# The product with w_out by seven block products in place of eight

## The chip, the cores and the metric

The kernel runs on one core of a Trainium2 chip. The metric is the device time of one launch in microseconds (us). Three runs of the kernel before took 3358.61, 3364.39 and 3369.11 us, a median of 3364.39 us. The engines are TensorE (PE: matmuls, with weight loads shown as PEld), VectorE (DVE), ScalarE (ACT), GpSimd (POOL) and SyncE (SP, which issues the DMAs).

## The reference

One layer of a diffusion backbone: a gated DeltaNet mixer on 2048 tokens of 1024 channels, then a channel mixer, then a final norm. The change lies in the channel mixer, whose hidden width is 2816 = 22 tiles of 128 channels:

```python
def conv_glu(h, w_in, conv_w, conv_b, w_out):
    val, gate = jnp.split(h @ w_in, 2, axis=-1)
    gate = dw_conv(gate, conv_w) + conv_b            # three taps along the tokens
    return (val * jax.nn.silu(gate)) @ w_out

x_lat = x_lat + mod_l[5] * conv_glu(h_lat, ffn_w_in[i], ffn_conv_w[i], ffn_conv_b[i], ffn_w_out[i])
return rms_norm(x_lat, final_norm_g)
```

All of it is float32. The kernel multiplies float32 matrices by splitting each operand into a rounded part and a remainder and adding three matmuls (`mm3`, L837): hi·hi, hi·lo and lo·hi.

## The kernel before

**Order of the work.** Every operation is recorded with its engine, an assumed cost, a priority and the buffer slots it takes (`Plan.op`). A list scheduler then writes out one order for each engine, from assumed costs and latencies; each engine runs its list in that order and waits at each instruction for its data and buffers. A late instruction so holds all that stands behind it on its engine.

**Forming an operand** (`form`, L1739) is a cast on ScalarE (L1752, the rounded part) and a subtraction on VectorE or GpSimd (L1755, the remainder). Formed stationary tiles take one of seven `wf` slots, moving operands one of fourteen `bf` slots; raw loads take one of four `raw3` slots, strictly in the order of recording (`load3`).

**The two windows of hidden channels** (`ffn_window`). A window is 1024 tokens. It goes over 11 pairs g of channel tiles. Each pair takes seven gate products (convolution and silu follow) and then seven value products; a product is 12 matmuls into one PSUM bank. The seven products already replace eight block products: `channels` (L1830) forms seven sums of weight blocks, four of them by GpSimd combines (L1850), and `products3` (L1861) adds the results. In the order of its VectorE instructions: the addition of the second product (`big<-fps,pc`, L1957), two additions that make u2 and u4 (`pc<-fps,pc`, L1904), one that makes u3, and then L1957 three times. The first of these three frees the bank of the third product, which the seventh product uses again. After a pair's value products GpSimd multiplies value by silu(gate) in two instructions of 1024 tokens (L2002), and SP stores both to DRAM (`hid_d`, L2005).

**The product with w_out** (`ffn_out`). For each half of the 1024 output columns and for blocks of four tiles of 128 tokens (the last block of the second half in two pieces), it runs over the 11 pairs: two formed channel tiles of the block (`wf`), times the two formed weight tiles (`bf`), added in four PSUM banks. A step of one channel tile on four token tiles is 12 matmuls. The weights of a half are formed once, in its first block. The first half is scaled, added to the residual and stored (`half_out`); the second adds its own half, takes the norm of the row and writes the output (`finish_out`).

Of the kernel before, what the change touches and what calls it, by code (L numbers as in the profile page):

```python
# [18 lines left out]
P = 128  # L19
# [227 lines left out]
class Kernel:  # L247
# [7 lines left out]
    def setup(self):  # L255
# [6 lines left out]
        self.hid_d = [dp.tile([P, 2, SEQ], F32, name=f"hid_d{g}") for g in range(NF // 2)]  # L262
        self.comb_d = [[dp.tile([P, 4, WB], F32, name=f"comb_d{w}{k}") for k in range(4)] for w in range(2)]
        self.y_d = [dp.tile([P, WB], F32, name=f"y_d{c}") for c in range(SEQ // P)]
# [1413 lines left out]
    def plan3(self):  # L1678
# [5 lines left out]

        nc, pl = self.nc, self.plan
# [36 lines left out]
        self.hid_done = {}  # L1722
# [208 lines left out]
    def ffn_window(self, w):  # L1931
# [12 lines left out]
        def hidden(g, prio):  # L1944
# [46 lines left out]
            vals = [[], []]  # L1991
            V = self.channels(g, 0, prio - 20)
            self.products3(V, B, prio, block_put(v_, v0), vals)
            for f in range(2):
                def ends(f=f):
                    if w:
                        nc.gpsimd.tensor_copy(v_[f].t[:, 0:1], carry(f, 2, 3))
                    else:
                        nc.gpsimd.tensor_copy(carry(f, 2, 3), v_[f].t[:, N - 1:N])

                def times(f=f):
                    nc.gpsimd.tensor_tensor(v_[f].t[:, :n], v_[f].t[:, :n], a_[f].t[:, :n], ALU.mult)  # L2002

# [4 lines left out]
                a = pl.op("POOL", 2.4, times, [e, acts[f]], prio, uses=[v_[f], a_[f]])  # L2008
                self.hid_done.setdefault(w, []).append(pl.op("SP", 1.5, store, [a], prio, uses=[v_[f]]))
# [3 lines left out]

    def ffn_out(self):


        nc, pl, T = self.nc, self.plan, self.ffn_t
        TT, TS = nc.vector.tensor_tensor, nc.vector.tensor_scalar
        base = 3000
        m5, fg, junk = (Buf("braw") for _ in range(3))  # L2020
        flat = lambda b: b.t.rearrange("p a b -> p (a b)")
# [9 lines left out]
        a = pl.op("SP", 1.0, load_m5, self.m_done[1] + [self.b_load, self.open_c], base - 40, alloc=[m5, fg])  # L2031
# [3 lines left out]
        n_acc = 0  # L2035
        y_done = {}
        nj = NF // 2
        for half in range(2):
            ns = slice(half * WB, (half + 1) * WB)
            W = []  # L2040
            blocks = [[0, 1, 2, 3], [4, 5, 6, 7], [8, 9, 10, 11]] + ([[12, 13], [14, 15]] if half else [[12, 13, 14, 15]])
            for i, ts in enumerate(blocks):
                prio = base + 1000 * half + 100 * i
                t0, nt = ts[0] * P, len(ts)
                ps = [Buf((("inv", "inv", "sc", "sc"), ("zp", "zp", "tr", "tr"))[n_acc % 2][t]) for t in range(nt)]
                n_acc += 1
                a = None
                for j in range(nj):
                    p = prio + j - 25
                    if i == 0:  # L2050
                        raw, l = self.load3(
                            "raw3", [P, 2, WB], self.i["ffn_out"][2 * j:2 * j + 2, :, ns].rearrange("f p c -> p f c"), [], p
                        )
                        W.append(self.form(lambda raw=raw: raw.t, [2, WB], raw, [l], p, "bf", "DVE" if j % 2 else "POOL"))
                    deps = self.hid_done[0] + (self.hid_done[1] if t0 + nt * P > 2 * WB - 1 else [])
                    raw, l = self.load3("raw3", [P, 2, nt * P], self.hid_d[j][:, :, t0:t0 + nt * P], deps, p)
                    hids = [
                        self.form(lambda raw=raw, f=f: raw.t[:, f], [nt * P], raw, [l], p, "wf", "DVE") for f in range(2)
                    ]

                    def mms(f, j=j, hids=hids, ps=ps, nt=nt, W=W):
                        if j == 0 and f == 0:
                            for b in ps:
                                b.t = self.pp.tile([P, WB], F32, name="fy", tag=b.tag, bufs=2)
                        h, w = hids[f].t, W[j].t
                        for t in range(nt):
                            s = slice(t * P, (t + 1) * P)
                            self.mm3(
                                ps[t].t, h[:, 0, s], h[:, 1, s], w[:, 0, f, :], w[:, 1, f, :],
                                j == 0 and f == 0, j == nj - 1 and f == 1,  # L2070
                            )

                    for f in range(2):
                        first = j == 0 and f == 0
                        a = pl.op(
                            "PE", 0.684 * nt, lambda f=f, mms=mms: mms(f), [a, W[j].done, hids[f].done], prio + j,
                            alloc=ps if first else [], uses=[W[j], hids[f]] + ([] if first else ps),
                        )
                    if j == nj - 5:
                        near = a  # L2080
                for t, c in enumerate(ts):
                    if half == 0:
                        y_done[c] = self.half_out(prio + 20, c, ps[t], a, near, m5, m5_done)
                    else:
                        self.finish_out(prio + 20, c, ps[t], a, near, m5, fg, junk, [m5_done, fg_done, new_junk], y_done[c], i > 2)

    def half_out(self, prio, c, ps, done, near, m5, m5_done):
# [4 lines left out]
        def load():  # L2092
            self.new3(row, [P, D])
            nc.sync.dma_start(row.t[:, WB:], self.x1_d[c][:, :WB])

        l = pl.op("SP", 0.8, load, [near, self.x1_done[c]], prio - 10, alloc=[row])
        a = pl.op("DVE", 0.67, lambda: nc.vector.tensor_tensor(
            row.t[:, :WB], ps.t, m5.t[:, :WB], ALU.mult), [l, done, m5_done], prio, uses=[row, ps, m5])
        a = pl.op("POOL", 1.25, lambda: nc.gpsimd.tensor_tensor(
            row.t[:, :WB], row.t[:, :WB], row.t[:, WB:], ALU.add), [a], prio, uses=[row])  # L2100
        return pl.op("SP", 0.8, lambda: nc.sync.dma_start(self.y_d[c], row.t[:, :WB]), [a], prio, uses=[row])

    def finish_out(self, prio, c, ps, done, near, m5, fg, junk, ready, y_done, late):

        nc, pl = self.nc, self.plan
        row, tmp, st = Buf("big3"), Buf("pc"), Buf("st3")
        TS = nc.vector.tensor_scalar

        def load():
            self.new3(row, [P, D])  # L2110
            nc.sync.dma_start(row.t[:, :WB], self.y_d[c])
            nc.sync.dma_start(row.t[:, WB:], self.x1_d[c][:, WB:])

        def scaled():
            self.new3(tmp, [P, WB])
            nc.vector.tensor_tensor(tmp.t, ps.t, m5.t[:, WB:], ALU.mult)

        def square(k):
            if k == 0:
                self.new3(st, [P, 4])  # L2120
            s = slice(k * WB, (k + 1) * WB)
            nc.scalar.activation(junk.t[:, s], row.t[:, s], AF.Square, accum_out=st.t[:, k:k + 1])

        eng, add = ("DVE", nc.vector) if late else ("POOL", nc.gpsimd)
# [81 lines left out]
```

## Time and profile before

| | us |
|---|---|
| median of three runs | 3364.39 |
| the profiled execution | 3358.7 |
| its span, first to last instruction | 3357.0 |
| first matmul of the windows' products (`fps`) | 1985.6 |
| window 2 begins its products | 2439.0 |
| first matmul of the product with w_out | 2859.9 |
| last matmul of it starts | 3346.2 |

The profiled execution is 1.7 us longer than its span and 5.7 us shorter than the median of the runs. A busy share is that of an engine's instructions in a stretch; matmuls overlap, so their single durations add up to more than the time they take.

### The profile page before, as it was taken

How to read it: one execution, taken by the hardware profiler on the slowest of the kernel's cores; microseconds unless marked ns; L12 is line 12 of the kernel's file. 1: busy time of each engine (PE TensorE's matmuls, PEld its weight loads, DVE VectorE, ACT ScalarE, POOL GpSimd, SP SyncE). 2: the span in 40 equal slices, each digit the busy share in tenths (PEclk: the TensorE clock that was granted, in tenths of full speed). 3: DMA queues.
4: the chain of work that ended last, by engine and by line, in shares of the span. 5: the costliest groups of instructions: out<-in, count | busy, mean ns of one | idle time of the engine just before them, and what ended most of it. 6: DMA issues, size and time to landing. Idle time of an engine off the chain costs nothing.

```text
span 3357.0 us, 65714 instructions
## 1 busy us (share of the span) xinstructions
PE 3228.9 (96%) x23898; PEld 2815.0 (84%) x23898; DVE 2380.9 (71%) x4797; ACT 1785.7 (53%) x4773; POOL 1823.7 (54%) x2248
## 2 busy tenths in 40 slices
PE   7979999999999999999999999999999999999998
PEld 4978899999999988999987777888778888888887
DVE  6778788888898988888566578666766666523534
ACT  6548766676677777777545444333433333322332
POOL 6347677676777778777655435444554444201311
PEclk8999999999999999999999999999999999999999
DMA  7321122232322323222265685222332222634643
GB/s 254 134 68 57 39 84 86 81 103 71 108 75 82 97 84 91 69 83 63 85 196 181 213 307 188 75 76 94 121 118 76 76 88 87 196 122 155 206 157 132
DMA packets 221004, 392.55 MB, mean 117 GB/s; under 512 B 20353, under 2 KB 102009, under 8 KB 219656
## 3 DMA queue, kind: packets, MB, share of 16 engines
q1 hardware_dynamic: 220680, 388.34, 36.3%
q8 instruction: 189, 3.10, 0.4%
q14 instruction: 135, 1.11, 0.1%
HBM read 300.64 MB, written 87.63 MB: 116 GB/s over the span
## 4 chain that ended last, share of the span: by engine, by line
PE 76%; DVE 14%; ACT 3%; DMA 3%; POOL 2%; issue 2%; SPq 0%; DVEq 0%; POOLq 0%; ACTq 0%
PE fps L841 8%; PE fps L839 8%; PE fps L840 8%; PE zps L839 6%; PE zps L840 5%; PE zps L841 5%; PE fy L840 5%; PE fy L841 5%; PE fy L839 5%; DVE acc L896 4%; PE scps L1253 3%; PE scps L1271 2%; PE scps L1280 2%; PE gqps L1093 2%; DVE blk L911 1%
## 5 line engine op out<-in xcount | busy, mean ns | idle before, releaser
L839 PE MATMUL zps<-hhl,wt 128*128 128x260 f32 (+1 forms) x2176 | 695.1, 319 | 8.3 <-DVE acc L896 6.7
L1752 ACT CAST wf<-raw 128x512 fp32r<-128x512 f32 (+1 forms) x506 | 302.0, 601 | 733.8 <-PE fps L841 292.4
L1755 DVE TENSOR_TENSOR wf<-raw,wf 128x512 fp32r<-128x512 f32 (+1 forms) x506 | 402.9, 803 | 361.7 <-ACT wf L1752 352.8
L840 PE MATMUL zps<-hhl,wt 128*128 128x260 f32 (+1 forms) x2176 | 617.8, 284 | 2.6 <-POOL hhl L967 2.6
L841 PE MATMUL zps<-hhl,wt 128*128 128x260 f32 (+1 forms) x2176 | 616.9, 284 | 0.0
L967 POOL TENSOR_TENSOR hhl<-hraw,hhl 128x260 fp32r<-128x260 f32 x568 | 427.7, 774 | 155.8 <-ACT hhl L963 153.4
L839 PE MATMUL fps<-bf,wf 128*128 128x512 f32 x1232 | 486.1, 395 | 14.6 <-ACT wf L1752 7.1
L841 PE MATMUL fps<-bf,wf 128*128 128x512 f32 x1232 | 485.6, 394 | 1.1 <-DVE wf L1755 1.1
L840 PE MATMUL fps<-bf,wf 128*128 128x512 f32 x1232 | 485.2, 394 | 0.0
L896 DVE SCALAR_TENSOR_TENSOR acc<-zps,convw,acc 128x256 f32<-128x256 f32 x832 | 399.1, 480 | 59.5 <-ACT acc L894 43.7
L839 PEld LDWEIGHTS zps<-hhl,wt 128*128 128x128 f32 x2176 | 415.5, 191 | 17.3 <-issue 11.2
L840 PEld LDWEIGHTS zps<-hhl,wt 128*128 128x128 f32 x2176 | 416.4, 191 | 3.3 <-POOL hhl L967 3.2
L841 PEld LDWEIGHTS zps<-hhl,wt 128*128 128x128 f32 x2176 | 413.3, 190 | 0.1
L1157 POOL TENSOR_TENSOR ct<-U,cst_lm 128x256 f16<-128x256 f16 x432 | 303.0, 722 | 62.4 <-PE inv L1164 50.4
L1187 ACT CAST yz<-inv 128x256 f16<-128x256 f32 x864 | 275.1, 380 | 83.3 <-PE inv L1181 80.5
L1850 POOL TENSOR_TENSOR raw<-raw 128x512 f32<-128x512 f32 x88 | 116.5, 1324 | 362.6 <-DVE wf L1755 354.2
L839 PEld LDWEIGHTS fps<-bf,wf 128*128 128x128 f32 x1232 | 232.4, 189 | 68.7 <-ACT wf L1752 7.5
L841 PEld LDWEIGHTS fps<-bf,wf 128*128 128x128 f32 x1232 | 232.2, 188 | 55.4 <-DVE wf L1755 2.4
L840 PEld LDWEIGHTS fps<-bf,wf 128*128 128x128 f32 x1232 | 232.3, 189 | 53.1 <-DVE bf L1755 0.3
L840 PE MATMUL fy<-bf,wf 128*128 128x512 f32 x704 | 276.4, 393 | 0.0
L841 PE MATMUL fy<-bf,wf 128*128 128x512 f32 x704 | 276.4, 393 | 0.0
L839 PE MATMUL fy<-bf,wf 128*128 128x512 f32 x704 | 276.3, 392 | 0.0
(251 smaller groups left out, 7602.2 us busy)
## 6 DMA issues: line engine op xcount, KB each, us to landing
hraw<-hT_d SPq DMA_DIRECT2D x284, 260.0 KB
raw<-in_ffn_in SPq DMA_DIRECT2D x88, 512.0 KB
raw<-hid_d SPq DMA_DIRECT2D x77, 512.0 KB
wmx<-in_w_mod SPq DMA_DIRECT2D x128, 128.0 KB
braw<-h_d SPq DMA_DIRECT2D x28, 512.0 KB
wt_st<-in_w_qkv SPq DMA_DIRECT2D x24, 512.0 KB
hid_d<-big SPq DMA_DIRECT2D x22, 512.5 KB
raw<-in_ffn_out SPq DMA_DIRECT2D x22, 512.0 KB
```

The source lines that it names most:

```text
L839: mm(out, lh, rh, start=first, stop=False)
L840: mm(out, lh, rl, start=False, stop=False)
L841: mm(out, ll, rh, start=False, stop=last)
L896: nc.vector.scalar_tensor_tensor(acc.t, ps.t[:, k:k + TB], wk, acc.t, ALU.mult, ALU.add)
L967: nc.gpsimd.tensor_tensor(t[:, 1, k], raw[q].t[:, k], t[:, 0, k].bitcast(F32), ALU.subtract)
L1093: mm(gq.t[:, c, :w, :], blk.t[:, c, 0, :], blk.t[:, c, 0:w, :], start=True, stop=True)
L1157: nc.gpsimd.tensor_tensor(col_sets(ct, lb, LATE), col_sets(U.t[:, 0], lb, LATE), v3(self.lm[:, li]), ALU.mult)
L1187: nc.scalar.copy(col_sets(yz.t[:, k], lb, sets), v3(ps.t[:, k]))
L1253: nc.tensor.matmul(ps.t[:, k, :], blk.t[:, ci, k, :], S.t, start=True, stop=True)
L1752: nc.scalar.copy(f.t[:, 0], src())
L1755: (nc.vector if eng == "DVE" else nc.gpsimd).tensor_tensor(f.t[:, 1], src(), f.t[:, 0].bitcast(F32), ALU.subtract)
L1850: return pl.op("POOL", 1.25, lambda: nc.gpsimd.tensor_tensor(part(*out), part(*a), part(*b), op), deps, prio, uses=[raw[k] for k in {out[0 ...
```

## The change

The hidden tokens A and the weights w_out are cut in two by token halves, even and odd channel tiles, and column halves. Seven products of sums of such blocks then give all four blocks of the result. What is stored to DRAM are seven operands `a_d[0..6]`: A11, A12, A22, A21+A22 and three more sums. GpSimd makes two of a pair's sums and VectorE two more in the second window (`sums`), after the first window's part is loaded again. The sums of weight blocks are made on GpSimd in the first window (`column_sums`, four subtractions of 512 columns for each pair) and stored to `t_d`. `ffn_out` then has seven steps of two blocks of four token tiles (the last block in two pieces), each over 11 channel tiles; the results are added in eight held tiles `C`, which take eight of the fourteen `bf` slots, so that six are left for a step's weights.

```diff
+        self.a_d = [dp.tile([P, NF // 2, 2 * WB], F32, name=f"a_d{k}") for k in range(7)]
+        self.t_d = [dp.tile([P, NF // 2, 2, WB], F32, name=f"t_d{k}") for k in range(2)]
...
                 def store(f=f):
-                    nc.sync.dma_start(self.hid_d[g][:, f, t0:t0 + n], v_[f].t[:, :n])
+                    if w:
+                        nc.sync.dma_start(self.a_d[f][:, g, N - 1:N], v_[f].t[:, 0:1])
+                    else:
+                        nc.sync.dma_start(self.a_d[f][:, g, :n], v_[f].t[:, :n])
...
+            if w:
+                sums(g, prio, v_, a_[0], timed, acts)
+            else:
+                self.column_sums(g, prio)
+
+        def sums(g, prio, v, s, timed, acts):
+            r = [Buf("braw") for _ in range(2)]
+            V = [lambda f=f: v[f].t[:, 1:1 + N] for f in range(2)]
...
+            l = pl.op("SP", 1.5, load, [acts[-1], *first], prio, alloc=r)
+            e = [pl.op("POOL", 0.1, lambda f=f: last(f), [l, timed[f]], prio, uses=[r[f], v[f]]) for f in range(2)]
+            a = pl.op("POOL", 2.4, lambda: nc.gpsimd.tensor_tensor(s.t[:, :N], V[0](), V[1](), ALU.add), timed, prio, uses=[s, *v])
+            put(2, V[1], a, [v[1]])
+            put(3, lambda: s.t[:, :N], a, [s])
+            b = pl.op("POOL", 2.4, lambda: nc.gpsimd.tensor_tensor(V[0](), r[0].t, V[0](), ALU.subtract), [a, *e], prio, uses=[r[0], v[0]])
+            put(5, V[0], b, [v[0]])
+            c = pl.op("DVE", 1.2, lambda: TT(r[0].t, s.t[:, :N], r[0].t, ALU.subtract), [b], prio, uses=[r[0], s])
+            put(4, lambda: r[0].t, c, [r[0]])
+            self.last_sum = pl.op("DVE", 1.2, lambda: TT(r[1].t, r[1].t, r[0].t, ALU.subtract), [c, *e], prio, uses=r)
+            put(6, lambda: r[1].t, self.last_sum, [r[1]])
...
+    def column_sums(self, g, prio):
...
+        def less(out, a, b, deps):
+            (i, j), x, y = out, a, b
+            return pl.op("POOL", 1.25, lambda: nc.gpsimd.tensor_tensor(
+                r[i].t[:, j], r[x[0]].t[:, x[1]], r[y[0]].t[:, y[1]], ALU.subtract), deps, prio, uses=r)
...
     def ffn_out(self):
+        steps = [
+            (0, w_part(0, 0), [(None, 2)]),
+            (1, w_part(1, 0), [(2, 0)]),
+            (4, t_part(1, 1), [(2, 2)]),
+            (3, t_part(0, 0), [(2, 3)]),
+            (6, w_part(1, 1), [(3, 1)]),
+            (5, t_part(0, 1), [(3, 3), (2, 2)]),
+            (2, t_part(1, 0), None),
+        ]
+        for s, (k, part, adds) in enumerate(steps):
+            for j in range(0, nj, 2):
+                raw, l = self.load3("raw3", [P, jj, WB], part(j, jj), self.t_done, prio + j - 15)
+                W.append(self.form(lambda raw=raw: raw.t, [jj, WB], raw, [l], prio + j - 15, "bf", "POOL" if j % 4 else "DVE"))
+            blocks = [range(4), range(4, 8)] if adds else [range(4), range(4, 6), range(6, 8)]
+            for i, ts in enumerate(blocks):
+                ps, a = self.products_out(prio + 30 * i, k, W, ts)
...
```

The rest of the new code adds a block's result from PSUM to `C` on VectorE (ScalarE copies in the first step); in the fifth and sixth step GpSimd scales a finished row and adds the residual (`plus_x`, two instructions of 1024 columns), and `finish` normalises and writes it.

What the change does to the order is shown at three places. On VectorE, in the second window, where the gate products of a pair begin (`wf` rows are L1755 before and L1757 after, and so on). Before:

```order
L1957 TENSOR_TENSOR big30_39197<-fps_39169,pc1_39178 128x512
L1755 TENSOR_TENSOR wf4_39195<-raw31_38999,wf4_39195 128x512
L1755 TENSOR_TENSOR wf5_39213<-raw30_39019,wf5_39213 128x512
L1904 TENSOR_TENSOR pc2_39231<-fps_39206,pc1_39178 128x512
L1904 TENSOR_TENSOR pc0_39235<-fps_39188,pc2_39231 128x512
L1755 TENSOR_TENSOR wf6_39233<-raw30_39019,wf6_39233 128x512
```

After:

```order
L1959 TENSOR_TENSOR big30_37591<-fps_37561,pc1_37570 128x512
L1757 TENSOR_TENSOR wf4_37589<-raw31_37386,wf4_37589 128x512
L2045 TENSOR_TENSOR braw3_37460<-big35_37384,braw3_37460 128x1024
L2047 TENSOR_TENSOR braw0_37462<-braw0_37462,braw3_37460 128x1024
L1757 TENSOR_TENSOR wf3_37610<-raw30_37406,wf3_37610 128x512
L1906 TENSOR_TENSOR pc2_37630<-fps_37603,pc1_37570 128x512
L1906 TENSOR_TENSOR pc0_37634<-fps_37582,pc2_37630 128x512
L1757 TENSOR_TENSOR wf2_37643<-raw30_37406,wf2_37643 128x512
L1906 TENSOR_TENSOR pc1_37654<-fps_37623,pc2_37630 128x512
L1959 TENSOR_TENSOR big31_37656<-fps_37582,pc1_37654 128x512
```

The two sums of the pair before (L2045, L2047) stand between the second and the third subtraction of the next set of weights, ahead of u2 and u4. On GpSimd, at the same place after the change:

```order
L2004 TENSOR_TENSOR big32_37508<-big32_37508,big33_37418 128x1025
L2032 COPY braw0_37462<-big32_37508 128x1
L2040 TENSOR_TENSOR big35_37384<-big34_37451,big32_37508 128x1024
L2043 TENSOR_TENSOR big34_37451<-braw3_37460,big34_37451 128x1024
L1852 TENSOR_TENSOR raw30_37406<-raw30_37406 128x512
L1852 TENSOR_TENSOR raw30_37406<-raw31_37386,raw30_37406 128x512
```

Before, the combines followed on the second multiplication (L2004, there L2002) at once; now two sums of 1024 columns stand between. On GpSimd in the first window, late, after the change (L2065 are the subtractions of weight columns; the first row is the last combine for the value products, the last the first combine for the next gate products):

```order
L1852 TENSOR_TENSOR raw31_34369<-raw31_34369 128x512
L2065 TENSOR_TENSOR braw2_34614<-braw2_34614 128x512
L2065 TENSOR_TENSOR braw2_34614<-braw1_34616,braw2_34614 128x512
L2065 TENSOR_TENSOR braw1_34616<-braw1_34616,braw2_34614 128x512
L1975 MEMSET big30_34584 128x1
L1976 COPY carry_31234<-big30_34584 128x2
L2065 TENSOR_TENSOR braw1_34616<-braw1_34616 128x512
L1975 MEMSET big31_34652 128x1
L1976 COPY carry_31234<-big31_34652 128x2
L2065 TENSOR_TENSOR braw2_34720<-braw2_34720 128x512
L2065 TENSOR_TENSOR braw2_34720<-braw1_34722,braw2_34720 128x512
L2065 TENSOR_TENSOR braw1_34722<-braw1_34722,braw2_34720 128x512
L1852 TENSOR_TENSOR raw33_34561<-raw33_34561 128x512
```

Before, none stood in this gap but the two memsets and two copies; now there are up to seven subtractions.

## Rows read from the trace of the kernel before

**Rows 1.** The page: busy time of TensorE, and its granted clock in 40 slices.
```profile
PE 3228.9 (96%) x23898; PEld 2815.0 (84%) x23898; DVE 2380.9 (71%) x4797; ACT 1785.7 (53%) x4773; POOL 1823.7 (54%) x2248
...
PEclk8999999999999999999999999999999999999999
```
**Rows 2.** Stretches: us, busy time of each engine, clock, DMA share, GB/s.
```profile
2439.00:2859.00 420.00, 419.31 (x1809) 340.90 (x1810) 278.20 (x355) 158.44 (x225) 197.69 (x172) 0.99 0.27 89
2859.60:3346.60 487.00, 487.00 (x2114) 396.61 (x2112) 205.04 (x293) 145.72 (x270) 82.33 (x55) 1.00 0.49 161
3346.60:3357.00 10.40, 0.02 (x1) 0.00 (x0) 5.42 (x12) 1.44 (x4) 1.10 (x2) 0.60 0.27 101
```
**Rows 3.** Waits of TensorE from 2000 us on: total, times, longest.
```profile
PE fps L839 <- ACT wf L1752: 7.1, 1, 7.1
PE fps L839 <- DVE big L1957: 5.0, 1, 5.0
PE fps L839 <- DVE pc L1904: 2.4, 2, 1.3
```
**Rows 4.** One tile, fy: duration ns min/median/max, first and last start.
```profile
L841 PE MATMUL fy<-bf,wf x704: 388/393/400, 2860.3 to 3346.2; 128*128 128x512 f32 x176
```
**Rows 5.** Timeline of GpSimd in window 2: start, duration, instruction, idle before.
```profile
2548.24 2.84 POOL L2002 TENSOR_TENSOR big<-big,big 128x1025 f32<-128x1025 f32 x1 [1.20 <-DVE big L1957]
...
2551.75 2.42 POOL L2002 TENSOR_TENSOR big<-big,big 128x1025 f32<-128x1025 f32 x1
2559.87 1.29 POOL L1850 TENSOR_TENSOR raw<-raw 128x512 f32<-128x512 f32 x1 [5.71 <-DVE wf L1755]
...
2579.24 1.29 POOL L1850 TENSOR_TENSOR raw<-raw 128x512 f32<-128x512 f32 x1 [12.79 <-DVE wf L1755]
```
**Rows 6.** Timeline of VectorE, same place.
```profile
2550.12 0.69 DVE L1957 TENSOR_TENSOR big<-fps,pc 128x512 f32<-128x512 f32 x1 [1.32 <-PE fps L841]
...
2553.55 1.16 DVE L1755 TENSOR_TENSOR wf<-raw,wf 128x512 fp32r<-128x512 f32 x1 [1.93 <-ACT wf L1752]
2555.72 0.69 DVE L1957 TENSOR_TENSOR big<-fps,pc 128x512 f32<-128x512 f32 x1 [1.01 <-PE fps L841]
2556.36 0.69 DVE L1755 TENSOR_TENSOR wf<-raw,wf 128x512 fp32r<-128x512 f32 x1
2559.10 0.69 DVE L1755 TENSOR_TENSOR wf<-raw,wf 128x512 fp32r<-128x512 f32 x1 [2.05 <-ACT wf L1752]
2561.12 1.42 DVE L1904 TENSOR_TENSOR pc<-fps,pc 128x512 f32<-128x512 f32 x2 [1.33 <-PE fps L841]
2562.46 0.68 DVE L1755 TENSOR_TENSOR wf<-raw,wf 128x512 fp32r<-128x512 f32 x1
2563.92 0.69 DVE L1904 TENSOR_TENSOR pc<-fps,pc 128x512 f32<-128x512 f32 x1 [0.78 <-PE fps L841]
2564.65 0.69 DVE L1957 TENSOR_TENSOR big<-fps,pc 128x512 f32<-128x512 f32 x1
```
**Rows 7.** Timeline of TensorE: first matmul of the seventh gate product.
```profile
2566.51 0.39 PE L839 MATMUL fps<-bf,wf 128*128 128x512 f32 x1
```
**Rows 8.** Groups of VectorE in window 2: count, busy us, mean ns, idle before.
```profile
L1981 DVE SCALAR_TENSOR_TENSOR big<-big,fcw,big 128x1025 f32<-128x1025 f32 x44 | 58.1, 1321 | 10.3 <-ACT big L1978 10.2
...
L2032 DVE TENSOR_TENSOR braw<-braw,braw 128x1024 f32<-128x1024 f32 x1 | 1.2, 1215 | 0.0
```
**Rows 9.** Timeline of ScalarE: the cast behind the first combine.
```profile
2561.20 0.62 ACT L1752 CAST wf<-raw 128x512 fp32r<-128x512 f32 x1 [2.13 <-POOL raw L1850]
```
**Rows 10.** Timeline in window 1, first pair: a slow multiplication and slow differences.
```profile
2033.47 3.39 POOL L2002 TENSOR_TENSOR big<-big,big 128x1023 f32<-128x1023 f32 x1
```
**Rows 11.** The same on VectorE.
```profile
2033.38 4.56 DVE L1798 TENSOR_TENSOR braw<-braw,braw 128x1024 f32<-128x1024 f32 x2
```
**Rows 12.** Waits between 2859.6 and 3346.6 us: total, times, longest.
```profile
ACT bf L1752 <- DMA raw<-in_ffn_out: 58.1, 18, 5.8
```

More of the change, by code (lines that the diff above doesn't have):

```diff
@@ L2009, in hidden, with load, last, put @@
-                self.hid_done.setdefault(w, []).append(pl.op("SP", 1.5, store, [a], prio, uses=[v_[f]]))
+                timed.append(pl.op("POOL", 2.4, times, [e, acts[f]], prio, uses=[v_[f], a_[f]]))
+                done = self.a_done.setdefault((f, g), [])
+                done.append(pl.op("SP", 1.5, store, [timed[f]], prio, uses=[v_[f]]))
+            if w:
[5 more added lines that the diff above has]
+            V = [lambda f=f: v[f].t[:, 1:1 + N] for f in range(2)]
+            def load():
+                for f in range(2):
+                    self.new3(r[f], [P, N])
+                    nc.sync.dma_start(r[f].t[:, :N - 1], self.a_d[f][:, g, :N - 1])
+            def last(f):
+                nc.gpsimd.tensor_copy(r[f].t[:, N - 1:N], v[f].t[:, 0:1])
+            def put(k, src, dep, uses):
+                self.a_done[k, g] = [pl.op("SP", 1.5, lambda: nc.sync.dma_start(self.a_d[k][:, g], src()), [dep], prio, uses=uses)]
+            first = [o for f in range(2) for o in self.a_done[f, g][:1]]
+            l = pl.op("SP", 1.5, load, [acts[-1], *first], prio, alloc=r)
[9 more added lines that the diff above has]
+            put(6, lambda: r[1].t, self.last_sum, [r[1]])
@@ L2087, in half_out, with w_part, t_part @@
-    def half_out(self, prio, c, ps, done, near, m5, m5_done):
+        ready = [m5_done, fg_done, new_junk]
+        self.n_acc = 0
+        nj, nt = NF // 2, SEQ // P // 2
+        C = [Buf("bf") for _ in range(nt)]
+        held = [[] for _ in range(nt)]
+        def w_part(f, n):
+            return lambda j, k: self.i["ffn_out"][2 * j + f:2 * j + f + 2 * k - 1:2, :, n * WB:(n + 1) * WB].rearrange("j p c -> p j c")
+        def t_part(f, n):
+            return lambda j, k: self.t_d[f][:, j:j + k, n]
@@ L2089, in half_out, with plus_x @@
+    def plus_x(self, prio, c, y, b, done, m5, ready):
         nc, pl = self.nc, self.plan
@@ L2101, in half_out @@
-        return pl.op("SP", 0.8, lambda: nc.sync.dma_start(self.y_d[c], row.t[:, :WB]), [a], prio, uses=[row])
-    def finish_out(self, prio, c, ps, done, near, m5, fg, junk, ready, y_done, late):
+            nc.sync.dma_start(row.t, self.x1_d[c])
+        flat = lambda: y.t[:, b:b + 2].rearrange("p a b -> p (a b)")
+        l = pl.op("SP", 1.5, load, [done, self.x1_done[c]], prio, alloc=[row])
+        a = pl.op("POOL", 2.5, lambda: nc.gpsimd.tensor_tensor(flat(), flat(), m5.t, ALU.mult), [done, *ready], prio, uses=[y, m5])
@@ L2105, in finish_out, with finish @@
+        return pl.op("POOL", 2.5, lambda: nc.gpsimd.tensor_tensor(flat(), flat(), row.t, ALU.add), [a, l], prio, uses=[row, y])
+    def finish(self, prio, c, y, b, done, ps, last, m5, fg, junk, ready, late):
         nc, pl = self.nc, self.plan
-        row, tmp, st = Buf("big3"), Buf("pc"), Buf("st3")
+        st = Buf("st3")
         TS = nc.vector.tensor_scalar
[L2109 to L2112, printed above, removed]
```

167 lines of the change are left out of this document (89 added, 78 removed).

## Prediction

> **What bounds the kernel now.** I read the page's busy line with the clock line first: TensorE is busy for 96% of the span, at 9 tenths or more of its clock in all slices but the first [rows 1]. Then the stretches around the change: in window 2 TensorE is busy for 419.3 of 420 us; in the product with w_out for all of 487.0 us, at clock 1.00, while VectorE has 205 us of work in it and GpSimd 82; 10.4 us of tail follow [rows 2]. Then its waits from 2000 us on: one of 7.1 us at the start of window 2, one of 5.0 and two of 2.4 together early in window 1 [rows 3]. So TensorE bounds all of this, and a matmul less is time won, as long as nothing else becomes late.
>
> A matmul's price is not its duration. Each of the three lines has 704 matmuls of 393 ns on the tile fy [rows 4], 2112 in all; 2112 x 0.393 would be 830 us, in a stretch of 487.0. They overlap; the price is the spacing, 487.0 / 2112 = 0.2306 us. Twelve matmuls (one product, or one channel tile on four token tiles) take 2.77 us, a block of 11 channel tiles 30.4 us.
>
> **The change part by part.**
>
> *Matmuls removed.* Seven steps x 8 token tiles x 11 channel tiles x 3 = 1848 in place of 2112: 264 x 0.2306 = 60.9 us less. The matmuls of both windows keep their order, so this is the whole of it on TensorE.
>
> *Sums in window 2.* Each pair adds two GpSimd and two VectorE instructions of 1024 columns. As sums of busy time they fit (window 2 has GpSimd at 198 and VectorE at 278 of 420 us [rows 2]), but they stand in a bad place: VectorE's list has both ahead of the next set's third subtraction, of u2 and of u4, so they hold what frees the bank for the seventh gate product. I follow that chain on the pair at 2550 us. Before: the second multiplication ends at 2554.2 [rows 5]; the third subtraction runs at 2559.10, u2 and u4 at 2561.12, then a fourth, u3 and the addition that frees the bank, done at 2565.34 [rows 6]; the seventh product starts at 2566.51 [rows 7]. The slack is 1.2 us.
>
> After: a subtraction of VectorE that starts at 2553.55 lasts 1.16 us where others last 0.69, and ends 0.5 us behind the multiplication [rows 5, 6]. I read this as the two engines taking turns. So the first sum starts at 2554.9 and takes 2.4, the price of the second multiplication [rows 5]: 2557.3. The subtraction that waits since 2556.36 goes next, 0.6. The second sum ends at 2560.3. VectorE's two sums take 1.22 each [rows 8]: 2562.8. The third subtraction: 2563.5. The first combine, 1.29 [rows 5]: 2564.9. The cast, 0.62 [rows 9]: 2565.5. The fourth subtraction waits for the second combine until 2566.2 and ends at 2566.8. Then u3 and the addition, 0.69 each: 2568.2. The seventh product starts some 0.1 later, 1.8 us behind 2566.51. Nothing gives this back, since TensorE has no idle time to save. Ten pairs have next gate products behind them (the eleventh's sums run beside the first step, whose banks they do not touch): 18 us.
>
> Bounds. If the engines do not take turns, the 0.1 and 0.6 us of waiting and the wait for the second combine fall away, the bank is free by 2566.4, and the loss is 0. At the slowest prices in the trace, 3.39 us for a multiplication [rows 10] and 2.28 for a difference [rows 11], half of the 4.56 that two take, the second sum ends at 2548.2 + 4 x 3.39 + 1.4 (what stands between them) = 2563.2, VectorE's at 2567.8, and the rest takes 5.3 us as above: 2573.1, 6.7 us late, 67 us over ten pairs. I take 18, from the rows nearest in time and place.
>
> The Trainium skill bears on this: "SBUF — State Buffer", section "SBUF: two separate sides", says that VectorE, with two SBUF inputs, and GpSimd lock one port pair against each other for a whole instruction, and the loser waits. By that rule the loss is the 18 us; were it mere sharing, 0 to 5. The 1.16 us subtraction agrees with the rule.
>
> The loads and stores: a pair goes from 6 DMA issues to 13. Behind the last two stores on SP stands a load of weights for the set after the next, wanted seven products, 19.4 us, later; that covers them. Cost 0; the few us by which such a load could be late lie in the bounds above.
>
> *Weight sums in window 1.* 44 GpSimd subtractions of 512 columns, priced as a combine, 1.29: 57 us in gaps of 12.8 us between two sets of combines (the idle time in the last of [rows 5]). Where four stand in a gap, they fit. By the order, seven do for two pairs: 7 x 1.29 = 9.0, and in the same gap VectorE has four taps of 1.32 [rows 8] and four subtractions of 0.6, 7.7 us in turn with them. 16.7 - 12.8 = 3.9 us late, less the slack of 1.2, makes 2.7 twice, 5 us. At the start of window 1 the differences for window 2 (L1798) leave VectorE's list, behind which TensorE waited 5.0 us [rows 3]; five subtractions come into GpSimd's list there, ahead of combines. I put this at 0, between 5 gained and 5 lost. Bounds: -5 to +15.
>
> *Seven sets of weights in place of two.* With eight `bf` slots held, a step's weights are formed in slots that the step before gives up in its last block: the first 2 x 2.77 = 5.5 us into it, so 24.9 us ahead of use. A load made ScalarE wait 5.8 us at worst in this stage [rows 12]; cast and subtraction take under 4 more. Hidden. If that cover went, six changes of step x 5.8 = 35 us. Only the first step is tight: all six weight loads stand ahead of its first tokens. I take 2, bounds 0 to 35.
>
> *Results added.* 48 additions from PSUM at 0.69 us on VectorE, at most eight in a block of 30.4 us, and on GpSimd 32 instructions of 2.4 us: both engines stay far under the 487 us stretch's length with the busy times above [rows 2]. The bank of a block is wanted again 30.4 us later. Cost 0; should it show, in single us.
>
> *Kept.* The last two token tiles end with the same operations as before: 10.4 us [rows 2]. At the start of window 2 the same loads stand behind the same stores on SP: the 7.1 us stay [rows 3].
>
> *Sum.* -60.9 + 18 + 5 + 2 = -35.9. The profiled execution took 3358.7 (span 3357.0 and 1.7 around it): 3322.8. The three timed runs have their median 5.7 above it, at 3364.4; I forecast the same place for the new kernel's: 3328.5, given as 3328.
>
> **The rivals.**
>
> *The sums are hidden.* VectorE had 1.9 and 2.1 us of idle before its subtractions there [rows 6], and half a microsecond at each of four links would do away with the loss. Then -60.9 + 2 to 5: 3364.4 - 58 = 3306. Against it: the 1.16 us row.
>
> *Slower: the sums in window 2 cost more than is won.* The mechanism is the chain above at the prices of window 1's first pair, which hold when more of VectorE's subtractions come between GpSimd's instructions than I count. Above 5.5 us for each of the ten pairs, that is with the second sum ending behind 2564, the change loses: 67 + 5 + 2 - 60.9 = +13, 3378. Against it: that pair had loads of window 2's operands beside it; later multiplications take 2.4 to 2.8.
>
> *The steps starve.* Weights come late at every change of step: -60.9 + 18 + 5 + 35 = -3, 3361. Against it: 24.9 us of cover. For it: two weight sets before were wanted once in 240 us, now one in 61.
>
> *Busy time is the price.* 264 x 0.393 = 104 us saved: 3364.4 - 104 + 25 = 3286. Against it: the spacing.
>
> **How the numbers follow.** Forecast 0.54, its own range 3316 to 3342; hidden 0.28; slower 0.08; starved 0.07; busy price 0.03. The range 3299 to 3355 leaves out the last, the slower case and most of the starved one. A measurement of this kernel can tell about 0.3%, 10 us, from no change. Faster by more: the forecast, hidden, busy price and a part of starved, 0.87. Within it: most of starved and the mild end of slower, 0.07. Slower: 0.06.
>
> **What would show it.** 616 matmuls on each of fy's three lines, with the spacing kept at 0.23 us in a stretch of some 426 us. In window 2, ten waits of TensorE of about 1.8 us each on VectorE's addition (now L1959), at a seventh gate product, and none elsewhere; the second GpSimd sum ending some 10 us behind the last value product, and VectorE's first sum waiting for it. If those waits are absent, the hidden case holds; waits of TensorE on casts or subtractions at the head of a step speak for starving. I am wrong if window 2 lengthens by under 5 or over 40 us, or if the stage of w_out lasts over 440 us.

## The result, and the profile after

The changed kernel takes 3343.2 us (median of four runs, 3339.9 to 3347.1), before it 3363.5: a ratio of 0.994, with an interval of 0.992 to 0.996. That is 20 us faster; 36 were forecast, and 3328 us. The time lies in the stated range of 3299 to 3355 us, and 1.2 us outside the forecast's own of 3316 to 3342; three terms of the sum do not lie where they were put.

The table holds the stages of all kernels, read from TensorE's matmuls: window 1 from the first matmul on the tile fps, window 2 from the end of a long wait near its start, the stage of w_out from the first fy to the start of the last. (Window 2 does not begin its products there, at 2439.0 us before the change, as the table ahead of the prediction has it: three of them stand ahead of that wait and are counted with window 1, in all kernels alike.) Window 1 starts at anything from 1980 to 2000 us, behind work that no experiment touches; a single time of 3340 says less than a stage. Each stage is read from one profile; kernels with the same work in a stage differ by up to 4.6 us in window 1, 2.1 in window 2 and 0.5 in w_out.

| kernel | median us | window 1 starts | window 1 | window 2 | w_out |
|---|---|---|---|---|---|
| before | 3363.5 | 1985.6 | 453.4 | 420.9 | 486.3 |
| changed | 3343.2 | 1985.4 | 475.5 | 426.6 | 441.5 |
| e1 no column sums | 3322.6 | 1984.3 | 454.8 | 426.7 | 441.9 |
| e2 no sums | 3344.9 | 1996.1 | 476.5 | 420.8 | 441.4 |
| e3 plus_x on VectorE | 3367.2 | 1999.1 | 479.1 | 426.8 | 463.8 |
| e4 column sums on VectorE | 3332.0 | 1989.9 | 468.1 | 427.3 | 441.7 |
| e5 column sums late | 3338.1 | 1987.5 | 469.1 | 426.4 | 441.7 |
| e6 column sums in w_out | 3359.2 | 1984.0 | 453.0 | 426.4 | 480.7 |
| e8 weights on VectorE | 3337.2 | 1979.9 | 475.9 | 425.4 | 439.6 |
| e9 plus_x later | 3361.3 | 1989.2 | 478.5 | 427.0 | 458.7 |
| e10 e6 paced, with e8 | 3345.7 | 1990.1 | 453.1 | 425.2 | 465.7 |
| e11 early half | 3336.7 | 1985.6 | 474.5 | 426.9 | 435.6 |
| e12 no plus_x | 3331.3 | 1999.9 | 475.4 | 426.9 | 425.7 |
| e13 paced, with e11 | 3320.6 | 1991.3 | 882.8 (both windows) | | 436.1 |

So between the two profiles window 1 grew by 22.1 us, window 2 by 5.7, and w_out shrank by 44.8 only.

The page after, TensorE, VectorE, GpSimd and the clock [rows 1]:
```profile
PE 3177.1 (95%) x23634; PEld 2762.4 (83%) x23634; DVE 2515.1 (75%) x4811; ACT 1782.0 (53%) x4752; POOL 2017.1 (60%) x2355
...
PEclk8989999999999999999999999999999999999999
```
TensorE has 264 matmuls less, as counted; GpSimd is busy 193 us longer, VectorE 134.

Window 2, the stage of w_out and the tail after (columns as in [rows 2]):
```profile
2460.90:2887.50 426.60, 423.48 (x1813) 341.01 (x1814) 324.78 (x374) 155.14 (x225) 250.86 (x214) 0.99 0.42 149
2887.50:3329.30 441.80, 431.49 (x1849) 348.58 (x1847) 261.90 (x288) 146.01 (x250) 154.79 (x77) 0.98 0.52 172
3329.30:3339.40 10.10, 0.10 (x1) 0.00 (x0) 5.52 (x12) 1.45 (x4) 1.10 (x2) 0.73 0.27 104
```
In w_out, where TensorE was busy in all 487.0 us before, it now idles for 10.3 of 441.8, at clock 0.98.

TensorE's waits from 2000 us on, after [rows 3]:
```profile
PE fps L840 <- DVE pc L1906: 25.6, 13, 7.4
PE fy L840 <- ACT wf L1754: 9.3, 2, 4.8
PE fps L840 <- ACT wf L1754: 6.6, 1, 6.6
PE fps L842 <- DVE wf L1757: 1.6, 2, 0.9
PE fy L842 <- DVE wf L1757: 0.9, 1, 0.9
```
The wait at the start of window 2 is kept (7.1, now 6.6). The 25.6 us on VectorE's additions, 23.6 of them in window 1, stand in place of 5.0 and 2.4; the 9.3 us at two changes of step are new.

The forecast's pair in window 2, after. GpSimd [rows 5]:
```profile
2575.10 2.40 POOL L2004 TENSOR_TENSOR big<-big,big 128x1025 f32<-128x1025 f32 x1
2577.56 0.53 POOL L2032 COPY braw<-big 128x1 f32<-128x1 f32 x1
2578.05 2.40 POOL L2040 TENSOR_TENSOR big<-big,big 128x1024 f32<-128x1024 f32 x1
2580.52 2.33 POOL L2043 TENSOR_TENSOR big<-braw,big 128x1024 f32<-128x1024 f32 x1
2586.05 1.30 POOL L1852 TENSOR_TENSOR raw<-raw 128x512 f32<-128x512 f32 x1 [3.20 <-DVE wf L1757]
```
VectorE [rows 6], and TensorE's seventh product [rows 7]:
```profile
2579.31 1.68 DVE L1757 TENSOR_TENSOR wf<-raw,wf 128x512 fp32r<-128x512 f32 x1
2582.88 1.23 DVE L2045 TENSOR_TENSOR braw<-big,braw 128x1024 f32<-128x1024 f32 x1 [1.89 <-POOL big L2043]
2584.14 1.22 DVE L2047 TENSOR_TENSOR braw<-braw,braw 128x1024 f32<-128x1024 f32 x1
2585.29 0.68 DVE L1757 TENSOR_TENSOR wf<-raw,wf 128x512 fp32r<-128x512 f32 x1
...
2588.04 1.24 DVE L1757 TENSOR_TENSOR wf<-raw,wf 128x512 fp32r<-128x512 f32 x1 [0.74 <-ACT wf L1754]
2589.20 0.68 DVE L1906 TENSOR_TENSOR pc<-fps,pc 128x512 f32<-128x512 f32 x1
2589.91 0.69 DVE L1959 TENSOR_TENSOR big<-fps,pc 128x512 f32<-128x512 f32 x1
```
```profile
2589.93 0.50 PE L840 MATMUL fps<-bf,wf 128*128 128x512 f32 x1 [0.30 <-DVE pc L1906]
```
The links are those that the forecast named, in its order and nearly at its prices. The second sum ends 5.4 us behind the second multiplication (6.1 forecast), and the product starts at the end of u3 (L1906), while L1959 has only just begun: u3 frees the bank, not the addition behind it. The description ahead of the prediction has that wrong. Those two make 1.5 of the 1.8 us; 0.30 of idle time are left.

### The profile page after: what moved, and what is told of

Read it like the earlier page. It is cut to its first block, busy times and chain, and to the rows that moved or that the text cites. A ratio compares the mean times of both kernels' runs of the same rounds, so it can differ in the third digit from the quotient of the medians.

```text
span 3339.4 us, 65439 instructions
## 1 busy us (share of the span) xinstructions
PE 3177.1 (95%) x23634; PEld 2762.4 (83%) x23634; DVE 2515.1 (75%) x4811; ACT 1782.0 (53%) x4752; POOL 2017.1 (60%) x2355
## 4 chain that ended last, share of the span: by engine, by line
PE 55%; DVE 16%; POOL 13%; issue 8%; DMA 5%; ACT 3%; SPq 0%; POOLq 0%; DVEq 0%; ACTq 0%
PE zps L840 6%; PE zps L841 5%; PE zps L842 5%; POOL raw L1852 4%; DVE acc L897 3%; PE fy L842 3%; PE fy L840 3%; PE fy L841 3%; PE scps L1254 3%; PE fps L840 3%; PE fps L842 3%; PE fps L841 3%; POOL big L2004 2%; PE scps L1272 2%; PE gqps L1094 2%
## 5 line engine op out<-in xcount | busy, mean ns | idle before, releaser
L1754 ACT CAST wf<-raw 128x512 fp32r<-128x512 f32 (+1 forms) x473 | 281.1, 608 | 663.2 <-POOL raw L1852 234.3
L1757 DVE TENSOR_TENSOR wf<-raw,wf 128x512 fp32r<-128x512 f32 (+1 forms) x473 | 456.3, 977 | 228.3 <-ACT wf L1754 226.5
L840 PE MATMUL fps<-bf,wf 128*128 128x512 f32 x1232 | 489.7, 397 | 32.5 <-DVE pc L1906 25.6
L842 PE MATMUL fps<-bf,wf 128*128 128x512 f32 x1232 | 487.0, 395 | 2.5 <-DVE wf L1757 2.5
L841 PE MATMUL fps<-bf,wf 128*128 128x512 f32 x1232 | 486.3, 395 | 0.0
L840 PE MATMUL fy<-bf,wf 128*128 128x512 f32 x616 | 244.1, 396 | 9.3 <-ACT wf L1754 9.3
L842 PE MATMUL fy<-bf,wf 128*128 128x512 f32 x616 | 243.6, 395 | 1.0 <-DVE wf L1757 0.9
L841 PE MATMUL fy<-bf,wf 128*128 128x512 f32 x616 | 243.4, 395 | 0.0
```

The costliest lines, as they stand in the source:

```text
L840: mm(out, lh, rh, start=first, stop=False)
L841: mm(out, lh, rl, start=False, stop=False)
L842: mm(out, ll, rh, start=False, stop=last)
L1754: nc.scalar.copy(f.t[:, 0], src())
L1757: (nc.vector if eng == "DVE" else nc.gpsimd).tensor_tensor(f.t[:, 1], src(), f.t[:, 0].bitcast(F32), ALU.subtract)
```

## The experiments

**e1, no column sums.** All of t comes straight from w_out.
```diff
-            else:
-                self.column_sums(g, prio)
...
+        t_part = w_part
```


> Leaves out the 44 subtractions of weight columns with their loads and stores; the three products that would read them read blocks of w_out of the same size, so the result is not the reference's. The trace of the changed kernel has window 1 at 475.5 us against 453.4 before. If the column sums cause that, by any path, window 1 falls to about 453 us and the time by 22, from 3343 to 3321 us. The forecast's term for them was 5 us: 3338. If window 1 is longer for another reason (stores to other tensors, say), the time stays near 3343.

Measured: window 1 at 454.8, the time 3322.6 (ratio to before 0.9877, 0.9862 to 0.9893). The column sums cost 20.7 us there, four times the term. (Four steps read other blocks, not three.)

**e2, no sums in window 2.** Lines L2040, L2043, L2045 and L2047 go.
```diff
-            a = pl.op("POOL", 2.4, lambda: nc.gpsimd.tensor_tensor(s.t[:, :N], V[0](), V[1](), ALU.add), ...
+            a = timed[1]
...
```


> Leaves out the two GpSimd and two VectorE sums of each pair in window 2; all loads and stores stay, of tensors that are not summed, so the result is not the reference's. The forecast's term was 18 us: 3325. Read from the trace of the changed kernel, window 2 is 426.4 us against 420.9 before, and TensorE's waits in it behind its first matmuls are 2 us in all: then at most 5.5 us go, 3338, and window 2 is about 421 us.

Measured: window 2 at 420.8, as before the change, so the sums cost 5.8 us. (The time, 3344.9, tells nothing: window 1 starts 10.7 us later in that profile.) TensorE idles for 0.04 us of that stage, against 2.0 us of waits in the changed kernel and 0.9 at its head. The other 2.9 us are in the starts of the matmuls: a matmul's row is 0.39 us long where starts lie 0.23 apart, so a start that is up to 0.16 us late shows no idle time. The pair behind the one above, changed kernel:
```profile
2628.73 0.40 PE L842 MATMUL fps<-bf,wf 128*128 128x512 f32 x1
2629.12 0.50 PE L840 MATMUL fps<-bf,wf 128*128 128x512 f32 x1
2629.46 0.39 PE L841 MATMUL fps<-bf,wf 128*128 128x512 f32 x1
```
Counted from start to start, the first two matmuls of the seventh gate product come late in ten pairs, by 0.16 to 0.59 us in a pair and 3.9 in all; the last pair's last value product comes 1.2 late, and the head of the stage loses 0.6 more than in e2. That is 5.7 of the 5.8 us, and the place is the forecast's.

**e3, plus_x on VectorE.**
```diff
-        a = pl.op("POOL", 2.5, lambda: nc.gpsimd.tensor_tensor(flat(), flat(), m5.t, ALU.mult), ...
+        a = pl.op("DVE", 1.2, lambda: nc.vector.tensor_tensor(flat(), flat(), m5.t, ALU.mult), ...
```


> plus_x's two instructions of 1024 columns go from GpSimd to VectorE. Theory: at the last two changes of step the weights' subtractions on GpSimd stand behind plus_x, the raw3 slots they hold keep the next tokens' loads back, and TensorE waits 4.8 and 4.5 us and runs at half its clock after. Then both waits go, the stage of w_out falls from 441.9 to about 427 us and the time to 3328. Rival: the weights come late by their loads or the bf slots, as the forecast's starving case had it; then the waits stay and the time is 3343, within 3.

Measured: 3367.2, and w_out at 463.8: neither. The first of the two waits fell from 4.8 to 2.1, but inside the sixth and seventh steps TensorE waited for a token's subtraction:
```profile
3230.45 0.80 PE L842 MATMUL fy<-bf,wf 128*128 128x512 f32 x1 [17.38 <-DVE wf L1757]
3308.48 0.80 PE L842 MATMUL fy<-bf,wf 128*128 128x512 f32 x1 [11.56 <-DVE wf L1757]
```
That subtraction stood behind plus_x and the normalising on VectorE's list. This moved the wait and told nothing of its cause.

**e5 and e4, the column sums late, and on VectorE.**
```diff
-                self.column_sums(g, prio)
+                self.column_sums(g, prio + 60)
```


> The column sums stay on GpSimd but begin some three pairs later, so that the differences for window 2 (L1800) stand where they stood before the change. Theory of displacement: the longest waits, 7.4 and 5.8 us in the first two pairs, come from those differences, which wait for their loads and for slots of braw that the column sums hold; then some 13 us and more go, window 1 is 460 us or less, and the time 3330 or less. Rival, turn-taking: each group of column subtractions slows VectorE's taps and the combines of the pair it stands in, wherever that is; then the waits move to later pairs and window 1 stays above 470 us, the time at 3340 to 3345.

Measured: window 1 at 469.1, 6.4 us less, between the two. The wait of 5.8 us in the second pair is gone; those of 6.8, 2.3, 3.2 and 2.9 are there. Displacement of the differences is the smaller part.
```diff
-            return pl.op("POOL", 1.25, lambda: nc.gpsimd.tensor_tensor(
+            return pl.op("DVE", 0.6, lambda: nc.vector.tensor_tensor(
```


> The 44 subtractions of weight columns go from GpSimd to VectorE, same loads and stores. Read by stages, since the work ahead of window 1 differs by up to 14 us from one profile to another: window 1 is 475.5 us now, 454.8 without column sums, 469.1 with them later. If the loss is GpSimd's time (its combines start later behind the column subtractions, and VectorE's instructions take turns with them), most of it goes: at 0.69 us each window 1 is 460 or less, the time some 3328. If it is the loads and stores of the column sums and the slots of braw, window 1 stays at 470 or more.

Measured: window 1 at 468.1, time 3332.0: between the two again. Neither engine alone nor the early position explains 20.7 us. What both kept was seen in the order only then: a list of work that is ready early is served early, and all 44 subtractions stand in the first five pairs.

**e6 and e10, the column sums in the stage of w_out.**
```diff
+        for g in range(NF // 2):
+            self.column_sums(g, base + 8 * g + 10)
...
```


> The column sums leave window 1 and stand on GpSimd in the first two steps of the stage of w_out, in slots of big3; only the steps that read them wait for their stores. GpSimd is busy for 63 of the first 305 us of that stage. Theory: window 1 falls to about 455 us and the stage of w_out stays at 442, so that the time is 3322. Rival: 11 loads of 1 MB beside tokens and weights, and 57 us of GpSimd ahead of weights' subtractions, make tokens or weights late: w_out at 450 us or more, the time above 3330.

Measured: window 1 at 453.0, but one wait of 36.5 us at the second step:
```profile
2960.75 0.79 PE L840 MATMUL fy<-bf,wf 128*128 128x512 f32 x1 [36.48 <-ACT wf L1754]
```
The rival held: the weights' loads stand behind column loads on SP (which waited 23.0 us there for stores of column sums to land), the weights' subtractions behind the column's on GpSimd. Paced by the products:
```diff
+            if self.n_col < 3 * nj:
+                if self.n_col % 3 == 0:
+                    self.column_sums(self.n_col // 3, prio + j + 1, a)
...
```


> The column sums stand in the first two steps of the stage of w_out again, but the loads of each wait for every third channel tile of the products there, one in 8.3 us, and the weights' subtractions are on VectorE. When they all stood at the head of that stage, window 1 fell to 453.0 us but TensorE waited 36.5 us at the second step, whose weights' loads stood behind theirs on SP and their subtractions behind theirs on GpSimd. Theory: paced, that wait goes; window 1 at 453 to 455, w_out at 440 to 445, the time 3320. Rival: the column loads and GpSimd's time cost the same wherever they stand, since they take turns with VectorE's subtractions: w_out at 455 or more, the time 3335 or more.

Measured: w_out at 465.7, with waits of 6.0 and 14.5 us early in it. Better than e6; but the stage is 26.1 us longer than in e8, which also has the weights' subtractions on VectorE, and that is more than window 1's loss: this stage has no room for them in this form. Which of loads and turns it is was not separated.

**e8 and e9, the weights' subtractions on VectorE, or ahead of plus_x.**
```diff
-... [l], prio + j - 15, "bf", "POOL" if j % 4 else "DVE"))
+... [l], prio + j - 15, "bf", "DVE"))
```


> All subtractions of the seven weight sets on VectorE; plus_x stays on GpSimd. With plus_x on VectorE the stage of w_out came out at 463.8 us, since VectorE's list then held the tokens' subtractions behind it. Theory: TensorE's waits at the last two changes of step (4.8 and 4.5) come from weights' subtractions on GpSimd behind plus_x; then they go and the stage is 427 to 432 us, the time about 3330. Rival: what is late there is VectorE's list or the loads, by the four slots of raw3; then the waits stay within 1 us of what they are, the stage at 441.

Measured: w_out at 439.6; the wait at the sixth step is gone, the one at the seventh is 6.4 us. What VectorE did beside plus_x there (e8, its timeline, then GpSimd's):
```profile
3225.43 4.87 DVE L2137 TENSOR_TENSOR bf<-bf,fy 128x512 f32<-128x512 f32 x8
3230.21 7.54 DVE L1757 TENSOR_TENSOR wf<-raw,wf 128x512 fp32r<-128x512 f32 x3
3237.68 3.43 DVE L1757 TENSOR_TENSOR bf<-raw,bf 128x1024 fp32r<-128x1024 f32 x1
```
```profile
3226.79 4.78 POOL L2192 TENSOR_TENSOR bf<-bf,braw 128x1024 f32<-128x1024 f32 x2 [3.93 <-DVE bf L2137]
3231.53 5.67 POOL L2193 TENSOR_TENSOR bf<-bf,big 128x1024 f32<-128x1024 f32 x2
3237.16 2.86 POOL L2192 TENSOR_TENSOR bf<-bf,braw 128x1024 f32<-128x1024 f32 x1
```
Eight additions that read a PSUM bank take 0.61 us each beside GpSimd; three subtractions of the same size with both inputs in SBUF take 2.5 each. The weight's subtraction at 3237.68 takes 3.43 us, one at 3257.20, behind plus_x, 1.23. So plus_x holds a weight's subtraction up on either engine: on GpSimd it stands ahead of it, on VectorE it slows it. Queueing plus_x of the fifth and sixth step behind the next step's weights (`later` is run once these are recorded):
```diff
-                        b = self.plus_x(prio + 30 * i + 20, t, C[t], 0, held[t][-1], m5, ready)
+                            b = self.plus_x(q, t, C[t], 0, h, m5, ready + formed)
...
```


> plus_x of the fifth and sixth step is queued on GpSimd behind the next step's weights in place of ahead of them. By the same theory the two waits go and the stage of w_out is 427 to 432 us, the time about 3330. Rival: plus_x and the normalising behind it crowd into the next step and hold VectorE's list there, as with plus_x on VectorE: waits inside a step, the stage at 441 or more.

Measured: w_out at 458.7. The sixth step starts without a wait, but one of 7.0 us stands in it, one of 9.3 at the seventh, five of 0.9 and one of 4.0 behind: the rival.

**e12 and e11, no plus_x, and half of it early.**
```diff
-        a = pl.op("POOL", 2.5, ... m5.t, ALU.mult), [done, *ready], prio, uses=[y, m5])
-        return pl.op("POOL", 2.5, ... row.t, ALU.add), [a, l], prio, uses=[row, y])
+        return pl.op("POOL", 0.1, lambda: nc.gpsimd.tensor_copy(y.t[:, b, :1], row.t[:, :1]), ...
```


> Leaves out plus_x's scaling and residual (32 GpSimd instructions of 1024 columns); their loads stay and a copy of one column keeps the order, so the result is not the reference's. Theory, plus_x in turns with the weights' subtractions: both waits go and the stage of w_out is 427 to 430 us, the time 3330. Rival, the loads or the six slots of bf are late by themselves: the waits stay, the stage at 437 or more.

Measured, the stage of w_out in e12:
```profile
2902.20:3328.20 426.00, 426.00 (x1849) 346.68 (x1847) 203.24 (x288) 146.93 (x250) 72.86 (x61) 1.00 0.55 179
```
No idle time, clock 1.00: 425.7 us, which is 616 x 3 x 0.2306 = 426.1. So plus_x, left out, takes all of the 15.8 us with it. VectorE's groups in the stage, changed kernel:
```profile
L1757 DVE TENSOR_TENSOR wf<-raw,wf 128x512 fp32r<-128x512 f32 x140 | 144.9, 1063 | 125.8 <-ACT wf L1754 125.6
...
L2137 DVE TENSOR_TENSOR bf<-bf,fy 128x512 f32<-128x512 f32 x48 | 29.5, 680 | 0.0
```
and in e12:
```profile
L1757 DVE TENSOR_TENSOR wf<-raw,wf 128x512 fp32r<-128x512 f32 x143 | 110.4, 797 | 151.7 <-ACT wf L1754 151.6
...
L2137 DVE TENSOR_TENSOR bf<-bf,fy 128x512 f32<-128x512 f32 x48 | 29.5, 678 | 0.0
```
The subtractions were 0.27 us longer each with plus_x beside them, the PSUM readers the same to 2 ns. In e11 the fifth step's half of it moves to the third step (`later` runs the edit once that step's weights are formed; `plus_half` is plus_x on 512 columns):
```diff
+                    if s == 1:
+                        def early(formed, q=prio + 100 + 30 * i, t=t, h=held[t][-1]):
+                            half[t] = self.plus_half(q, t, C[t], 0, h, m5, ready + formed)
...
+                        b = self.plus_half(prio + 30 * i + 20, t, C[t], 1, held[t][-1], m5, ready + [half[t]])
...
```


> Of the rows finished in the fifth step, the left half is scaled and gets its residual in the third step already (its sum is complete after the second), so that plus_x's time on GpSimd at the end of the fifth step halves; the sixth step's stays. Theory: plus_x on GpSimd takes turns with the subtractions of the next step's weights, which keeps their slots of raw3 and so the next tokens' loads back. Then the wait of 4.8 us at the sixth step goes or falls under 1, with some 1.5 us of lower clock, and the stage is 435 to 437 us. Rival: that wait has another cause; the stage stays at 441.

Measured: the first wait is gone, the second stays at 5.5 us, w_out at 435.6, as the theory had it.

**e13, one group of column sums a pair, with e11.** `prev` is the second multiplication of the pair before, `e` the last copy behind the gate's sums.
```diff
+            if not w and g > 1:
+                self.column_sums(g, prio, self.prev, e)
...
+                for c in {4: [0], 7: [1]}.get(g, []):
+                    self.column_sums(c, prio, acts[-1])
...
```


> All of the computation. Two changes. The column sums of window 1 are paced: in the changed kernel all 44 stand in the first five of its eleven pairs, up to twelve in one; here none stands in the first two pairs and four stand in each later one, in the gap behind the gate's combines (two further groups in the gap behind the value's combines), and the tokens of window 2 wait for their stores, so that the differences for window 2 stand where they stood before. And the early half of plus_x as in the run before, which brought the stage of w_out to 435.6 us. Theory, crowding: four fit in a gap, as the forecast had it, and the loss in window 1 is that of five crowded pairs; then window 1 is 454 to 458 us and the time 3317 to 3322. Rival, a price for each subtraction wherever it stands, by its turn with VectorE's taps: 20.7 us of window 1 for 44 is 0.5 each; then window 1 stays at 465 or more, the time at 3328 or more.

Measured: 3320.6 us (3318.5 to 3325.0), a ratio to before of 0.987 (0.985 to 0.989). Both windows together take 882.8 us, against 902.1 in the changed kernel and 881.5 in e1, which has no column sums at all. VectorE's taps in window 1, e13 and then e1:
```profile
L1983 DVE SCALAR_TENSOR_TENSOR big<-big,fcw,big 128x1023 f32<-128x1023 f32 x44 | 74.5, 1709 | 6.8 <-ACT big L1980 6.6
```
```profile
L1983 DVE SCALAR_TENSOR_TENSOR big<-big,fcw,big 128x1023 f32<-128x1023 f32 x44 | 57.2, 1300 | 8.0 <-ACT big L1980 7.9
```
The turns are all still paid, 0.41 us on each of 44 taps, more than in the changed kernel (1345 ns). But four subtractions in an idle gap make no one late, and TensorE has no new wait in window 1 (at the start of window 2 it has 8.4 us in three waits, in place of 6.6). Crowding was the loss, not turns as such. What of the crowding cost the time, the engines' time or the loads, stores and slots of `braw`, was not separated: e13 paces them all at once, and in e4, with GpSimd rid of the subtractions, 13.3 of the 20.7 us stayed.

## Why the prediction was right or wrong

*Matmuls removed*, -60.9. Right: without plus_x the stage is 425.7, which is 60.6 less than 486.3. The spacing of 0.2306 us is kept; busy time is not the price.

*Sums in window 2*, +18. Too large: 5.8 (e2). The chain was the right one: the seventh gate product comes late in all ten pairs, by 3.9 us in place of 18. The step that failed is the bank: it is free at the end of u3, so the slack on the pair before was 1.9 us (from 2564.61 to 2566.51 [rows 6, 7]) and not 1.2; the second sum also came 0.7 earlier. (The upper bound took 2.28 us for a difference as a slowest price, from two that take 4.56 together; one by one these take 1.22 and 3.43.) By the rule of the Trainium skill, "SBUF — State Buffer", section "SBUF: two separate sides", the loss was to be 18; the rule itself agrees with e8 and e12, where, of the two groups compared, only the one with both inputs in SBUF was held up. A rule on each instruction does not give the loss: the slack does.

*Weight sums in window 1*, +5. The term that failed most: 20.7 (e1), beyond its bound of 15 (between the two profiles window 1 grew by 22.1, of which 1.4 stay in e1, within what its profiles differ by). Two steps are wrong. "Where four stand in a gap, they fit" is true (e13), but I charged two pairs with seven when the order had all 44 in the first five. And the start of the window, "I put this at 0", holds two waits in place of one of 5.0: 7.4 us in the first pair and 5.8 in the second. In the first, five column subtractions at 1.8 to 1.9 us each run ahead of the combine, which starts at 2026.91:
```profile
2016.65 1.76 POOL L2065 TENSOR_TENSOR braw<-braw 128x512 f32<-128x512 f32 x1
2018.49 3.85 POOL L2065 TENSOR_TENSOR braw<-braw,braw 128x512 f32<-128x512 f32 x2
2022.43 3.86 POOL L2065 TENSOR_TENSOR braw<-braw 128x512 f32<-128x512 f32 x2
2026.91 2.23 POOL L1852 TENSOR_TENSOR raw<-raw 128x512 f32<-128x512 f32 x1 [0.63 <-DVE wf L1757]
```
In the second, one of the displaced differences stands on VectorE's list ahead of u2 and u4 and waits 1.29 us for its load, issued behind stores of column sums on SP; another, of 2.28 us, stands ahead of u3:
```profile
2072.47 1.23 DVE L1800 TENSOR_TENSOR braw<-braw,braw 128x1024 f32<-128x1024 f32 x1 [1.29 <-DMA braw<-h_d]
2073.61 0.68 DVE L1757 TENSOR_TENSOR wf<-raw,wf 128x512 fp32r<-128x512 f32 x1
2074.21 1.41 DVE L1906 TENSOR_TENSOR pc<-fps,pc 128x512 f32<-128x512 f32 x2
...
2077.47 2.28 DVE L1800 TENSOR_TENSOR braw<-braw,braw 128x1024 f32<-128x1024 f32 x1
```
With the differences back in place (e5) 6.4 us return; with the crowding gone as well (e13), nearly all.

*Seven weight sets*, +2, and *results added*, 0. The two changes of step cost 15.8, where the sum had 2 and single us at most, by a mechanism priced at nothing: plus_x was counted as busy time on an engine with room. It runs just when the next step's weights are formed; their subtractions stand behind it on GpSimd or are slow beside it on VectorE, their slots of `raw3` stay taken, and the next tokens' loads stand behind them on SP. At the sixth step, changed kernel, GpSimd, SP, ScalarE and TensorE:
```profile
3186.24 2.40 POOL L2193 TENSOR_TENSOR bf<-bf,big 128x1024 f32<-128x1024 f32 x1
3188.60 5.62 POOL L1757 TENSOR_TENSOR bf<-raw,bf 128x1024 fp32r<-128x1024 f32 x2
```
```profile
3189.22 3.16 SPq L2233 DMA_DIRECT2D out<-bf  x2
3192.47 2.15 SPq L1774 DMA_DIRECT2D raw<-a_d  x2
```
```profile
3196.00 1.14 ACT L1754 CAST wf<-raw 128x512 fp32r<-128x512 f32 x2 [5.23 <-DMA raw<-a_d]
```
```profile
3196.67 0.79 PE L840 MATMUL fy<-bf,wf 128*128 128x512 f32 x1 [4.83 <-ACT wf L1754]
```
The first step, called the tight one, had no wait. Shown is that plus_x is the cause (e12, e11); that the held slots are the path is read from rows and was not tried by itself. At the seventh step they fit it: the subtraction on GpSimd ends at 3260.09, the tokens' load is issued at 3260.11. At the sixth there is a second holder: the subtraction ends at 3191.47, but on SP two stores of finished rows (L2233), which wait for VectorE's normalising, stand ahead of the tokens' load, and it is issued at 3192.47, right behind them. Stores and normalising hang on plus_x too, so e12 and e11 do not tell the two paths apart.

*Kept*, tail and start of window 2: 10.1 us and 6.6, right.

With the measured sizes the sum of the spans is -60.6 + 5.7 + 22.1 + 15.8 and -0.6 for the tail (-0.4, counted from the start of the last fy) and where window 1 starts (-0.2): -17.6, which is 3339.4 - 3357.0. That the time lies in the range is in part luck: one term was too large by 12 us, two too small by 17 and 14, and the range was wide enough for what they left. By its own marks the prediction is wrong at one (w_out at 441.5, over 440) and barely inside at another (window 2 longer by 5.7). Of the rivals none came; the starved one's place was right (the change of step), its price and cause were not.

## What to carry to other kernels

Work that depends on nothing is served as soon as its engine is free, however late it is wanted: read from the order where all of it lands before pricing it gap by gap, and pace it by a dependency on work of the place where it fits. Busy time of GpSimd is not its cost: ask which instructions of VectorE with both inputs in SBUF run beside it, and what waits for those. On a chain of small waits, find the instruction that frees the resource, since slack of half a microsecond decides.

## What the runs showed of the hardware

A wait can cost twice. After the wait of 4.83 us at the sixth step TensorE's granted clock (changed kernel, columns as in [rows 2]) was at its lower level, 1.2 GHz, and then rose:
```profile
3196.60:3200.00 3.40, 3.26 (x7) 2.17 (x8) 3.40 (x6) 1.93 (x5) 2.27 (x2) 0.50 0.99 342
3200.00:3204.00 4.00, 4.00 (x17) 3.23 (x16) 4.00 (x3) 0.48 (x2) 4.00 (x2) 0.89 0.97 305
3204.00:3210.00 6.00, 6.00 (x27) 4.79 (x26) 6.00 (x4) 2.07 (x4) 5.14 (x3) 1.00 0.99 389
```
After a wait of 3.69 us in window 1 (at 2165.41) it was 0.68 for 3.4 us and 0.84 for 4 more; after one of 2.85 there (at 2208.95) it stayed at 1.00. In w_out 10.2 us of waits stand beside 15.8 of loss. Counted from start to start of the matmuls, TensorE lost 7.3 us at the sixth step and 8.1 at the seventh, with what followed each wait; the lower clock is most of the difference, by an estimate from the first two rows 3.4 x 0.50 + 4.0 x 0.11 = 2.1 us at the sixth step.
